# Up projections of the two branches: four PSUM banks, two low halves on another engine, a subtraction one tile later, and a later place for the residual rows

## The chip, the cores and the metric

The kernel runs on one core of a Trainium2 chip. Its engines work side by side, each through its own list of instructions in order: TensorE (PE: matmuls, which write to PSUM), VectorE (DVE), ScalarE (ACT), GpSimd (POOL) and SyncE (SP). They wait for one another by semaphores. DMAs are issued from SP's queue and from POOL's queue. PSUM has eight banks of 128 x 512 float32. The metric is the time of one execution on the device, in microseconds; three runs of the kernel before took 800.81 to 802.07 us, with a median of 801.13.

## What is computed

One decoder layer on x of 512 x 1024 in float32. After a norm, one wide projection gives the inputs of two branches: an mLSTM (`hm`, 512 x 512) and a sparse attention (`on`, 512 x 512), and two gates `gm` and `gn` of 512 x 1024. The branches are projected up, gated, added and projected by `w_out`; the result is added to x (the residual), normalised again and sent through a gated MLP with a short convolution. The part around the change:

```
y = jax.nn.sigmoid(gm + merge_gate_b[0]) * (hm @ w_up_m) \
    + jax.nn.sigmoid(gn + merge_gate_b[1]) * (on @ w_up_n)
x = x + y @ w_out
h2 = rmsnorm(x, norm2_w)
```

`w_up_m` and `w_up_n` are 512 x 1024, `w_out` is 1024 x 1024.

## The kernel before

**Products in three matmuls.** Every float32 operand of a large product is split into a high half in TensorE's rounded format (fp32r) and a low half, the rest. A product is H·h + H·l + L·h, three matmuls. So each weight has to be converted: `Weights.ensure(i)` (L71 and on) takes half i of a loaded chunk, writes its high half with a copy on ScalarE (L88), and the low half in one of two ways. In the usual way VectorE subtracts high from raw (L94). For halves listed in `W.on_dma`, ScalarE writes the negative of the high half (L91) and a DMA from POOL's queue adds the raw weights to it in place (L92). The second way takes more of ScalarE and a transfer, and nothing of VectorE.

**Order of the weights.** Chunks are loaded from SP's queue (L68) into two raw buffers in turn; a chunk is loaded as soon as `ensure` comes to the first half of the chunk before it, and waits on the queue until the buffer's last reader is done. For a half converted by DMA, that reader is the DMA. The converted halves lie in four buffers in turn. `w_up_n`, `w_up_m` and `w_out` have four, four and eight halves, and the text calls them UN0 to UN3, UM0 to UM3 and WO0 to WO7; two halves make a chunk. The list `PLAN` holds switches; `poolUN` is 2, so all four halves of `w_up_n` go the way with the DMA; those of `w_up_m` and `w_out` go through VectorE.

**Streams of projection work.** The order of all instructions on each engine is that of the program. A `Filler` takes a generator of matmul steps (three matmuls, valued at 650) and issues as many as the surrounding stage asks for, so that TensorE has products between the small operations of the other stages. An evacuation of a finished PSUM tile is put into the program two steps after the tile's last step (`after(2, ...)`).

**The two up projections.** `up_group` works through eight tiles m of 128 x 512, each of four steps, twelve matmuls; a pair of tiles needs one half of the weights. At the third step of every even tile it calls `ensure` for the half three places on. The `un` group runs beside the last head of the mLSTM: the products `mo` (L1136), which wait for `EA` (L1128), the norm of that head, then the sigmoids of `gn` on ScalarE (L1275, between two loads of function tables, L1271 and L1276), and, after 18 steps, the four transposes `mhT` (L1165). A `un` tile is evacuated by a multiply into `gn` (L741) on VectorE. The `un` group uses the two `pa` banks in turn. The `um` group then uses the two `psS` tiles in turn, which the mLSTM heads used before (two banks each, of which `um` takes the first).

**The merge.** `evac_um(m)` multiplies a `um` tile into `gm` (L1299), adds `gn` (L1300), both on VectorE (`umpool` is 0), copies to the high half `yH` on ScalarE (L1301), and subtracts for the low half `yL` on VectorE (L1302).

**What comes behind.** The PSUM pool of the stages so far is closed and a pool of eight single banks takes its place; a bank of it waits for the last reader of the old tile at that place. Each of the eight k-steps of `w_out` goes over four row tiles and two column halves: 24 matmuls into eight banks. The residual rows (four loads of 512 KB, L1289) and the weights of the second norm (L1291) are issued from POOL's queue ahead of the `um` group, into pages of the pool `outer`, which held the normalised input until the last `gn` product. Their sum with the `w_out` product (L1346), the norm and the MLP follow.

Of the kernel before, what the change touches and what calls it, by code (L numbers as in the profile page):

```python
# [15 lines left out]
P = 128  # L16
S = 512
D = 1024
NT = S // P
KD = D // P  # L20
# [77 lines left out]
def bcast(ap, n):  # L98
    return bass.AP(tensor=ap.tensor, offset=ap.offset, ap=[[0, P], [1, n]])
# [17 lines left out]
    "p_sc21": 0, "p_sc30": 0, "p_sc31": 1, "poolA": 2, "poolC": 0, "poolGM": 2, "poolGN": 2, "poolMO": 2,  # L117
    "poolMQK": 2, "poolMV": 0, "poolUM": 0, "poolUN": 2, "poolWO": 0, "q2_eb": 1, "q2_ex0": 0, "q2_ex1": 0,
# [10 lines left out]
def FL(key, default):  # L129
    return PLAN.get(key, default)  # L130


PD = dict(A=0, C=2, MV=2, GM=2, MO=2, MQK=2, GN=0, UN=0, UM=0, WO=0)
# [27 lines left out]
def body(ctx, tc, I, out, dbg=None):  # L161
    nc = tc.nc
    act, dve, pe, pool = nc.scalar, nc.vector, nc.tensor, nc.gpsimd
    ctx.enter_context(tc.manual_schedule())

    x = I["x"][0]
# [30 lines left out]
    def page(name, dt=F32):  # L197
        return ar.tile([P, 2048], dt, name=name, tag="pg", bufs=PG)
# [7 lines left out]
    def s4(name, dt=F32):  # L206
        return ar.tile([P, 1024], dt, name=name, tag="s4", bufs=6)
# [13 lines left out]
    def v4(tl):  # L221
        return tl[:, :2048].rearrange("p (k t) -> p k t", t=S)

    def act4(tiles, k, a=0, b=S):
        return v4(tiles[k // 4])[:, k % 4, a:b]

    T = {}
# [10 lines left out]
    W = Weights(nc, wpool, 2, 4)  # L238
# [17 lines left out]
    def add_feat(src, c0, nkt, width, per_half):  # L256
        s = src[:, c0:c0 + width].rearrange("(k p) n -> p k n", p=P)
        views = [lambda v, a=a: v[:, :, a:a + per_half] for a in range(0, width, per_half)]
        return W.add((nkt, width), [(lambda v: v, s)], views)
# [9 lines left out]
    F_UN = [i for c in range(0, 1024, 512) for i in add_feat(w_up_n, c, 4, 512, 256)]  # L269
    F_UM = [i for c in range(0, 1024, 512) for i in add_feat(w_up_m, c, 4, 512, 256)]  # L270
# [20 lines left out]
    W.on_pool = {T_B[c] for c in range(4) if FL(f"q2_pb{c}", (1, 0, 0, 0)[c])}  # L291
    for nm, ids in (("A", T_A), ("C", T_C), ("MV", T_MV), ("GM", F_GM), ("MO", F_MO), ("MQK", F_MQK), ("GN", F_GN),
                    ("UN", F_UN), ("UM", F_UM), ("WO", T_WO[:4])):
        W.on_dma |= set(ids[1:len(ids):2] if FL("pool" + nm, PD[nm]) == 1 else ids if FL("pool" + nm, PD[nm]) == 2 else [])
    for i in T_WO[4:]:
        W.dst[i] = page_r

# [137 lines left out]
    def after(n, fn):  # L435
        later.append([n, fn])

    def tick():
        ready = []
        for e in later:  # L440
            e[0] -= 1
        while any(e[0] <= 0 for e in later):
            n = next(i for i, e in enumerate(later) if e[0] <= 0)
            ready.append(later.pop(n)[1])
        for fn in ready:
            fn()
# [48 lines left out]
                yield 650  # L495
                tick()

    def up_group(ids, mH, mL, evac, nm, flag, bank=pa):
        for m in range(KD):
            acc = bank(f"{nm}{m}")[:, 0:512]  # L500
            W.ensure(ids[m // 2])
            H, L = W.hl[ids[m // 2]]
            w = slice((m % 2) * P, (m % 2) * P + P)
            for k in range(4):
                if k == 2 and m % 2 == 0:
                    W.ensure(ids[m // 2] + 3)
                pe.matmul(acc, H[:, k, w], mH[:, k, :], start=(k == 0), stop=False)
                pe.matmul(acc, H[:, k, w], mL[:, k, :], start=False, stop=False)
                pe.matmul(acc, L[:, k, w], mH[:, k, :], start=False, stop=(k == 3))
                if k == 3:  # L510
                    after(2, lambda m=m, acc=acc: evac(m, acc))
                    if m == KD - 1:
                        after(2, lambda: done.add(flag))
                yield 650
                tick()
# [227 lines left out]
    def proj_stream():  # L743
        yield from tok_group(T_C, 288, tok_accs("aC"), evac_c, "C")
        yield from tok_group(T_A, 512, tok_accs("aA"), evac_a, "A")
        T["mv1"] = lpage("mv1").rearrange("p (t h c) -> p t h c", t=NT, h=4)
        pool.memset(T["mv1"][:, :, :, P:P + 1], 1.0)
        yield from tok_group(T_MV, 512, tok_accs("aV"), evac_mv, "MV")
        T["gm"] = [v4(opage(f"gm{i}")) for i in range(2)]
        yield from feat_group(F_GM, gate_evac("gm", 0), "gm", "GM")  # L750
        T["mo"] = v4(page("mo"))
        yield from feat_group(F_MO, evac_mo, "mo", "MO")
        yield from feat_group(F_MQK, evac_conv, "mqk", "MQK")
        T["gn"] = [v4(page(f"gn{i}")) for i in range(2)]
        yield from feat_group(F_GN, gate_evac("gn", 8), "gn", "GN")

    fill = Filler(proj_stream(), flush)
# [330 lines left out]
    def mls_s(h):  # L1088
        r0 = slice((h % 2) * 64, (h % 2) * 64 + 64)
        mq = T["mq"][h // 2][r0]  # L1090
        A = psS(f"mA{h}")
        B = psS(f"mB{h}")
        mb = B[:, 0:512]
        pe.matmul(mb, sel[:, h, :], T["nHL"], start=True, stop=True)
        at = [A[:, 0:512], A[:, 512:896], B[:, 768:1024], B[:, 512:768]]
        for j in range(NT):
            ks = slice(j * P, (j + 1) * P)
            kh, kl = mq[:, 1, ks], mq[:, 3, ks]

            q0 = min(j, NT - 2) * P  # L1100
            qh, ql = mq[:, 0, q0:], mq[:, 2, q0:]
            pe.matmul(at[j], kh, qh, start=True, stop=False)
            pe.matmul(at[j], kh, ql, start=False, stop=False)
            pe.matmul(at[j], kl, qh, start=False, stop=True)
        return A[:, 0:896], B[:, 640:1024], mb
# [20 lines left out]
    def mls_m(sc, ee):  # L1126
        EA, EB, et = ee
        dve.scalar_tensor_tensor(EA, sc[0], 0.125, EA, op0=ALU.mult, op1=ALU.mult)  # L1128
        dve.scalar_tensor_tensor(EB, sc[1], 0.125, EB, op0=ALU.mult, op1=ALU.mult)
# [119 lines left out]
    for i in range(2):  # L1249
        for z in range(2):  # L1250
            g = T["gm"][i][:, 2 * z:2 * z + 2, :]
# [9 lines left out]
    for h in range(4):  # L1261
        if h < 3:
            mid = (lambda: mls_s(h + 1), lambda n: mls_e(h + 1, n), mls_x)
        else:
            mid = (lambda: None, lambda n: None, lambda n: None)
        fill(FL(f"mb{h}", 1000))
        hs, sc, ee = mls_b(h, ee[2], mid)
        if h == 3:
            fill.until(done, "GN")
            fill = Filler(up_group(F_UN, T["onH"], T["onL"], evac_un, "un", "UN"), flush)  # L1270
            act.preload_act_table_set("sigmoid_and_others")  # L1271
            for i in range(2):
                for z in range(2):
                    g = T["gn"][i][:, 2 * z:2 * z + 2, :]
                    act.activation(g, g, AF.Sigmoid)  # L1275
            act.preload_act_table_set(LNEXP)  # L1276
        fill(FL(f"mc{h}", 5000))
        mls_c(h, hs)
        if h < 3:
            fill(FL(f"md{h}", 2000))  # L1280
            mls_m(sc, ee)
# [3 lines left out]
    x1p = [opage(f"x1_{i}") for i in range(2)]  # L1285
    x1d = dram.tile([S, D], F32, name="x1d")
    x1 = [x1p[t // 2][:, (t % 2) * 1024:(t % 2) * 1024 + 1024] for t in range(NT)]
    for t in range(NT):
        pool.dma_start(x1[t], x[t * P:(t + 1) * P, :])  # L1289
    nw2 = s4("nw2")  # L1290
    pool.dma_start(nw2, bcast(I["norm2_w"], D))  # L1291


    yH = [page(f"yH{i}", F32R) for i in range(2)]
    yL = [lpage("yL0", F32R), page("yL1", F32R)]

    def evac_um(m, a):
        g = T["gm"][m // 4][:, m % 4, :]
        dve.tensor_mul(g, g, a)  # L1299
        (pool if m < FL("umpool", 5) else dve).tensor_add(g, g, T["gn"][m // 4][:, m % 4, :])  # L1300
        act.activation(act4(yH, m), g, AF.Copy)  # L1301
        dve.tensor_sub(act4(yL, m), g, act4(yH, m))  # L1302

    fill = Filler(up_group(F_UM, T["hmH"], T["hmL"], evac_um, "um", "UM", psS), flush)
    fill(1e9)
    ps_cm.close()

# [6 lines left out]
    acc = {t: [pf(f"wo{t}{c}") for c in range(2)] for t in range(NT)}  # L1314

    def wo(i, t):
        H, L = W.hl[T_WO[i]]
        for c in range(2):
            mm3(acc[t][c], act4(yH, i, t * P, (t + 1) * P), act4(yL, i, t * P, (t + 1) * P),
                H[:, 0, c * 512:(c + 1) * 512], L[:, 0, c * 512:(c + 1) * 512], i == 0, i == KD - 1)  # L1320

    for i in range(4):
        W.ensure(T_WO[i])
        for t in range(NT):
            if t == 2:
                W.ensure(T_WO[i] + 3)
            wo(i, t)
    W.ensure(T_WO[7])
    h2H = [opage_r(f"h2H{i}") for i in range(2)]
    h2L = [opage_r(f"h2L{i}") for i in range(2)]  # L1330
# [144 lines left out]
    acc = {}  # L1475
# [53 lines left out]
    for j in range(2, NJ - 2):  # L1529
# [7 lines left out]
        if 4 <= j < 8:  # L1537
            t = j - 4
# [102 lines left out]
```

## Time and profile before

| | us |
|---|---|
| median of three runs | 801.13 |
| the profiled execution, own time | 799.94 |
| its span, first to last instruction | 798.2 |
| TensorE busy | 776.9 (97%) |
| VectorE busy | 469.7 (59%) |
| ScalarE busy | 373.0 (47%) |
| GpSimd busy | 211.1 (26%) |

Busy time is the sum of an engine's instructions, loads of weights into TensorE's array apart. Starts are in us from the first instruction. In a row of the timeline the square bracket says how long the engine stood before the instruction and what released it; several equal instructions in a row are merged, with their count behind an x. The duration of a matmul is longer than the distance to the next one, since they overlap; the pace is read from starts. Instructions of VectorE and ScalarE overlap by a little too.

### The profile page before, as it was taken

The page shows a single profiled execution, that of the slowest core. Times are in us where ns is not written, and L with a number is a line of the kernel's source. Part 1 is how long each engine was busy: PE and PEld are TensorE (multiplying, and loading weights), DVE is VectorE, ACT ScalarE, POOL GpSimd, SP SyncE. Part 2 cuts the span into 40 slices and gives each one's busy share as a digit, 9 for nine tenths or more (in the row PEclk, how much of TensorE's full clock was granted, in tenths as well). Part 3 has the DMA queues.
Part 4 walks back from the last instruction along what each step waited for, and adds up shares of the span by engine and source line. Part 5 has one row for each costly group of instructions (what it writes and reads, how often), then busy time and mean ns, then how long its engine had stood idle before and what let it go on. Part 6 is the DMA issues. An engine that isn't in the chain of part 4 may idle for free.

```text
span 798.2 us, 10535 instructions
## 1 busy us (share of the span) xinstructions
PE 776.9 (97%) x4037; PEld 640.9 (80%) x4037; DVE 469.7 (59%) x825; ACT 373.0 (47%) x629; POOL 211.1 (26%) x219
## 2 busy tenths in 40 slices
PE   8999989999999999988999999999999999999998
PEld 5897878778788878866778998888888888888886
DVE  5476875686565654534764545555545544466865
ACT  6353546645565596571343343343343343355541
POOL 5320121220111122121000009855554444200600
PEclk9999999999999999999999999999999999999999
DMA  7884158665555567348343427675454444485472
GB/s 234 290 222 133 25 135 132 109 113 96 106 106 107 106 106 129 83 106 263 105 151 125 148 106 290 241 260 209 182 188 181 188 158 159 168 306 177 144 233 93
DMA packets 94371, 127.98 MB, mean 160 GB/s; under 512 B 6479, under 2 KB 73199, under 8 KB 92912
## 3 DMA queue, kind: packets, MB, share of 16 engines
q1 hardware_dynamic: 63054, 91.64, 34.3%
q0 software_dynamic: 31264, 35.66, 21.6%
q8 instruction: 32, 0.52, 0.3%
q14 instruction: 19, 0.16, 0.1%
q10 hardware_dynamic: 2, 0.00, 0.0%
HBM read 94.79 MB, written 15.73 MB: 138 GB/s over the span
## 4 chain that ended last, share of the span: by engine, by line
PE 79%; DVE 9%; ACT 6%; DMA 3%; issue 2%; SPq 0%; DVEq 0%; ACTq 0%
PE ff L1356 10%; PE ff L1357 10%; PE ff L1358 10%; PE P L426 4%; PE P L427 4%; PE P L425 4%; PE on L946 2%; PE ptp L935 2%; PE wo L425 2%; PE wo L426 2%; PE wo L427 2%; PE gm L487 1%; PE gm L489 1%; PE gm L488 1%; PE sp L905 1%
## 5 line engine op out<-in xcount | busy, mean ns | idle before, releaser
L94 DVE TENSOR_TENSOR whl<-raw,whl 128x1024 fp32r<-128x1024 f32 (+1 forms) x110 | 138.9, 1276 | 146.7 <-ACT whl L88 146.7
L88 ACT ACTIVATE whl<-raw 128x1024 fp32r<-128x1024 f32 (+2 forms) x144 | 144.8, 1013 | 125.7 <-PE ff L1358 57.0
L1356 PE MATMUL ff<-h2H,whl 128*128 128x512 f32 (+1 forms) x384 | 142.8, 372 | 0.0
L1357 PE MATMUL ff<-h2L,whl 128*128 128x512 f32 (+1 forms) x384 | 142.6, 371 | 0.0
L1358 PE MATMUL ff<-h2H,whl 128*128 128x512 f32 (+1 forms) x384 | 142.6, 371 | 0.0
L92 POOL DMA_DIRECT2D whl<-raw x32 | 46.2, 1444 | 198.5 <-ACT whl L91 190.3
L1358 PEld LDWEIGHTS ff<-h2H,whl 128*128 128x128 f32 x384 | 72.3, 188 | 12.6
L1356 PEld LDWEIGHTS ff<-h2H,whl 128*128 128x128 f32 x384 | 72.3, 188 | 12.5
L1357 PEld LDWEIGHTS ff<-h2L,whl 128*128 128x128 f32 x384 | 72.3, 188 | 12.3
L920 ACT ACTIVATE P<-sp,nmx 128x128 f32<-128x128 f32 (+3 forms) x64 | 33.1, 524 | 36.7 <-DVE nmx L911 36.4
L1408 ACT ACTIVATE ct<-ct 128x512 f32<-128x512 f32 x22 | 14.0, 634 | 54.4 <-DVE ct L1406 54.4
L911 DVE TENSOR_REDUCE nmx<-sp 128x2 f32<-128x256 f32 (+3 forms) x32 | 26.2, 818 | 17.9 <-PE sp L908 17.8
L426 PE MATMUL P<-whl,g 128*128 128x512 f32 x88 | 34.2, 389 | 0.0
L427 PE MATMUL P<-whl,g 128*128 128x512 f32 x88 | 34.2, 389 | 0.0
L425 PE MATMUL P<-whl,g 128*128 128x512 f32 x88 | 34.2, 389 | 0.0
L1406 DVE SCALAR_TENSOR_TENSOR ct<-ff,vcol,ct 128x511 f32<-128x511 f32 (+1 forms) x44 | 32.8, 744 | 2.5 <-ACT ct L1404 1.7
L91 ACT ACTIVATE whl<-raw 128x1024 fp32r<-128x1024 f32 x32 | 33.6, 1050 | 0.0
L1414 ACT ACTIVATE g<-ct 128x512 fp32r<-128x512 f32 x22 | 13.9, 634 | 37.0 <-DVE ct L1418 21.9
L235 DVE COPY P<-ptp 128x256 f32<-128x256 f32 (+1 forms) x32 | 17.7, 554 | 19.3 <-PE ptp L935 19.2
L1415 DVE TENSOR_TENSOR g<-ct,g 128x512 fp32r<-128x512 f32 x22 | 15.4, 699 | 22.0 <-ACT g L1414 22.0
L425 PE MATMUL wo<-whl,yH 128*128 128x512 f32 x64 | 25.2, 394 | 1.8 <-DVE gm L1299 1.8
L487 PE MATMUL gm<-hTH,whl 128*128 128x512 f32 x64 | 26.6, 416 | 0.0
(400 smaller groups left out, 1788.6 us busy)
## 6 DMA issues: line engine op xcount, KB each, us to landing
raw<-in_ffn_w_up_dram SPq DMA_DIRECT2D x22, 1024.0 KB, 5.0
raw<-in_w_in_dram SPq DMA_DIRECT2D x16, 1024.0 KB, 5.0
whl<-raw POOLq DMA_DIRECT2D x32, 512.0 KB, 5.7
st<-in_ffn_w_down_dram SPq DMA_DIRECT2D x11, 1024.0 KB, 6.9
td<-st POOLq DMA_DIRECT2D x11, 1024.0 KB, 4.1
raw<-td SPq DMA_DIRECT2D x22, 512.0 KB, 5.4
raw<-in_ffn_w_down_dram SPq DMA_DIRECT2D x11, 512.0 KB, 4.4
raw<-in_w_out_dram SPq DMA_DIRECT2D x4, 1024.0 KB, 11.0
```

The lines of the kernel that those rows point to most:

```text
L88: nc.scalar.activation(h, src, AF.Copy)
L91: nc.scalar.activation(l, src, AF.Copy, scale=-1.0)
L92: nc.gpsimd.dma_start(l, src, accum_op=ALU.add)
L94: (nc.gpsimd if n in self.on_pool else nc.vector).tensor_sub(l, src, h)
L425: pe.matmul(o, aH, bH, start=start, stop=False)
L426: pe.matmul(o, aH, bL, start=False, stop=False)
L427: pe.matmul(o, aL, bH, start=False, stop=stop)
L487: pe.matmul(acc, H[:, k, :], hh, start=(k == 0), stop=False)
L920: act.activation(Pv[:, y], sv[:, y], AF.Exp, bias=nmx[:, y:y + 1], accum_out=den[:, y:y + 1])
L1356: pe.matmul(acc[:, a:b], H[:, k, :], hh, start=(k == 0), stop=False)
L1357: pe.matmul(acc[:, a:b], H[:, k, :], hl, start=False, stop=False)
L1358: pe.matmul(acc[:, a:b], L[:, k, :], hh, start=False, stop=(k == KD - 1))
```

## The change

Five edits. First, `poolUN` becomes 3, a new value: the first two halves of `w_up_n` keep the DMA, UN2 and UN3 get their low half from VectorE. Second, `up_group` takes its PSUM tile for even m from `pa` and for odd m from `psS`, in both groups, so each goes over four banks. Third, UN3 is converted ahead of the sigmoids of `gn`, where it was behind them, by its own call of `ensure`. Fourth, `evac_um(m)` subtracts for the tile before, m - 1, and for the last tile both. Fifth, the loads of the residual rows and of the second norm's weights are issued in the program inside the first four steps of `w_out`, a row tile after each, where they were ahead of the `um` group; their pages are allocated at the old place.

```
-    "poolMQK": 2, "poolMV": 0, "poolUM": 0, "poolUN": 2, "poolWO": 0, ...
+    "poolMQK": 2, "poolMV": 0, "poolUM": 0, "poolUN": 3, "poolWO": 0, ...

-        W.on_dma |= set(ids[1:len(ids):2] if FL("pool" + nm, PD[nm]) == 1 else ids if FL("pool" + nm, PD[nm]) == 2 else [])
+        W.on_dma |= set(ids[1:len(ids):2] if FL("pool" + nm, PD[nm]) == 1 else ids if FL("pool" + nm, PD[nm]) == 2
+                       else ids[:2] if FL("pool" + nm, PD[nm]) == 3 else [])

-    def up_group(ids, mH, mL, evac, nm, flag, bank=pa):
+    def up_group(ids, mH, mL, evac, nm, flag):
         for m in range(KD):
-            acc = bank(f"{nm}{m}")[:, 0:512]
+            acc = (psS if m % 2 else pa)(f"{nm}{m}")[:, 0:512]

             fill = Filler(up_group(F_UN, T["onH"], T["onL"], evac_un, "un", "UN"), flush)
+            W.ensure(F_UN[3])
             act.preload_act_table_set("sigmoid_and_others")

-    for t in range(NT):
-        pool.dma_start(x1[t], x[t * P:(t + 1) * P, :])
     nw2 = s4("nw2")
-    pool.dma_start(nw2, bcast(I["norm2_w"], D))

         act.activation(act4(yH, m), g, AF.Copy)
-        dve.tensor_sub(act4(yL, m), g, act4(yH, m))
-
-    fill = Filler(up_group(F_UM, T["hmH"], T["hmL"], evac_um, "um", "UM", psS), flush)
+        if m:
+            y_low(m - 1)
+        if m == KD - 1:
+            y_low(m)
+
+    def y_low(m):
+        dve.tensor_sub(act4(yL, m), T["gm"][m // 4][:, m % 4, :], act4(yH, m))
+
+    fill = Filler(up_group(F_UM, T["hmH"], T["hmL"], evac_um, "um", "UM"), flush)

             wo(i, t)
+        pool.dma_start(x1[i], x[i * P:(i + 1) * P, :])
+        if i == 1:
+            pool.dma_start(nw2, bcast(I["norm2_w"], D))
```

## Rows read from the trace of the kernel before

**Rows 1.** TensorE by stretch: us, busy (matmuls), granted clock, DMA share, GB/s.
```profile
345.00:403.00 58.00, 49.15 (x207) 0.97 0.50 153
379.60:383.10 3.50, 3.48 (x9) 0.52 0.83 293
403.00:798.00 395.00, 391.30 (x1829) 1.00 0.53 187
```
**Rows 2.** Waits of TensorE from 335 to 440: us in total, times, longest.
```profile
PE un L507 <- DVE gn L741: 3.8, 3, 2.5
PE um L507 <- DVE gm L1299: 3.3, 2, 2.2
...
PE mo L1136 <- DVE EA L1128: 0.6, 1, 0.6
```
**Rows 3.** Timeline of TensorE, 344 to 403: start, us, instruction, idle before it.
```profile
344.80 0.47 PE L507 MATMUL un<-onH,whl 128*128 128x512 f32 x1
...
361.27 0.60 PE L1165 MATMUL mhT<-ident,hs 128*128 128x128 f32 x4
...
371.83 0.39 PE L507 MATMUL um<-hmH,whl 128*128 128x512 f32 x1
...
379.62 0.77 PE L507 MATMUL um<-hmH,whl 128*128 128x512 f32 x1 [2.18 <-DVE gm L1299]
...
399.02 0.39 PE L425 MATMUL wo<-whl,yH 128*128 128x512 f32 x1
...
400.83 0.39 PE L427 MATMUL wo<-whl,yL 128*128 128x512 f32 x1
402.99 0.50 PE L425 MATMUL wo<-whl,yH 128*128 128x512 f32 x1 [1.76 <-DVE gm L1299]
```
**Rows 4.** Timeline of ScalarE: UN2's first pass, UM0's, a merge copy, WO0's.
```profile
340.61 1.04 ACT L88 ACTIVATE whl<-raw 128x1024 fp32r<-128x1024 f32 x1
...
356.82 1.04 ACT L88 ACTIVATE whl<-raw 128x1024 fp32r<-128x1024 f32 x1
...
382.94 0.63 ACT L1301 ACTIVATE yH<-gm 128x512 fp32r<-128x512 f32 x1 [2.08 <-DVE gm L1300]
383.48 1.05 ACT L88 ACTIVATE whl<-raw 128x1024 fp32r<-128x1024 f32 x1
```
**Rows 5.** Timeline of VectorE: `EA` ahead of `mo`, and the first two `un` evacuations.
```profile
341.35 1.08 DVE L1128 SCALAR_TENSOR_TENSOR EA<-mA,EA 128x896 f32<-128x896 f32 x1
...
350.78 1.29 DVE L741 TENSOR_TENSOR gn<-gn,un 128x512 f32<-128x512 f32 x2 [0.18 <-ACT gn L1275]
```
**Rows 6.** Timeline of VectorE in the merge, 378.5 to 386.
```profile
378.79 0.68 DVE L1299 TENSOR_TENSOR gm<-gm,um 128x512 f32<-128x512 f32 x1
379.50 0.69 DVE L1300 TENSOR_TENSOR gm<-gm,gn 128x512 f32<-128x512 f32 x1
380.89 0.69 DVE L1302 TENSOR_TENSOR yL<-gm,yH 128x512 fp32r<-128x512 f32 x1 [0.70 <-ACT yH L1301]
381.50 0.68 DVE L1299 TENSOR_TENSOR gm<-gm,um 128x512 f32<-128x512 f32 x1
...
384.56 1.23 DVE L94 TENSOR_TENSOR whl<-raw,whl 128x1024 fp32r<-128x1024 f32 x1 [0.26 <-ACT whl L88]
385.70 0.68 DVE L1299 TENSOR_TENSOR gm<-gm,um 128x512 f32<-128x512 f32 x1
```
**Rows 7.** POOL's queue, UN1, UN3, residual rows; landing of L92's 32 DMAs.
```profile
339.93 1.29 POOL L92 DMA_DIRECT2D whl<-raw  x1 [1.55 <-ACT whl L91]
...
357.29 1.28 POOL L92 DMA_DIRECT2D whl<-raw  x1 [13.11 <-ACT whl L91]
358.04 2.71 POOL L1289 DMA_DIRECT2D x<-in_x_dram  x4
...
DMA to landing us min/median/max: 4.4/5.7/9.6
```
**Rows 8.** DMA issues from 363 to 364: KB each, us to landing.
```profile
raw<-in_w_up_m_dram SPq DMA_DIRECT2D x1, 1024.0 KB, 10.7
```

More of the change, by code (lines that the diff above doesn't have):

```diff
@@ L117 @@
     "p_sc21": 0, "p_sc30": 0, "p_sc31": 1, "poolA": 2, "poolC": 0, "poolGM": 2, "poolGN": 2, "poolMO": 2,
-    "poolMQK": 2, "poolMV": 0, "poolUM": 0, "poolUN": 2, "poolWO": 0, "q2_eb": 1, "q2_ex0": 0, "q2_ex1": 0,
+    "poolMQK": 2, "poolMV": 0, "poolUM": 0, "poolUN": 3, "poolWO": 0, "q2_eb": 1, "q2_ex0": 0, "q2_ex1": 0,
     "q2_ex2": 1, "q2_ex3": 0, "q2_na": 1, "q2_nb": 1, "q2_nc": 1, "q2_pb0": 1, "q2_pb1": 1, "q2_pb2": 0,
```

## The prediction

> **What bounds the kernel now.** The table of stages comes first [rows 1]: TensorE is busy 391.30 of the 395 us from 403 to the end, but only 49.15 of the 58 us from 345 to 403, the two up projections and the first products of `w_out`. So what this change can give back lies in those 58 us. The waits of TensorE say who holds it there [rows 2]: the `un` products wait 3.8 us for the evacuation of an older bank (`gn`, L741), the `um` products 3.3 us for theirs (L1299), and `mo`, just ahead, 0.6 us for `EA`. The timeline of TensorE gives the places [rows 3]: `un` begins at 344.80, `um` at 371.83, `um` stands 2.18 us until 379.62, the first `w_out` product is issued at 399.02, and its fourth bank has to wait until 402.99 for the last `um` evacuation. From there on TensorE runs through, so **the start of that matmul, 402.99, is the point that counts**: what moves it moves the end. The nine matmuls from 399.02 to 400.83 give the pace, 1.81/8 = 0.227 us each, 2.72 us for a tile of twelve, 5.44 us for two. Eight tiles need 21.8 us; `un` took 27.03.
>
> **UN2 (third half of `w_up_n`): low half on VectorE.** Its high half runs on ScalarE from 340.61 for 1.04 us [rows 4], and so the new subtraction can start at 341.7. By program order it stands before `EA`, which today starts at 341.35 [rows 5]. One such subtraction takes 1.14 us until the next instruction (384.56 to 385.70 [rows 6]). `EA` then starts at 341.7 + 1.14 = 342.84, which is 1.5 us later, and `mo` waits for just that instruction. Bounds: 0, if something else were late by as much, and 1.5; I take 1.5, since the wait on `EA` is already there. `un` begins at 346.3. ScalarE loses its second pass over UN2, which nobody waits for.
>
> **UN3: before the sigmoids, low half on VectorE.** Its high half costs ScalarE one more pass of 1.0 us ahead of the sigmoids' table load. The first evacuation of `un` today starts at 350.78, released by a sigmoid [rows 5]; it comes at 350.78 + 1.5 + 1.0 = 353.3. With two banks that would stall the third tile. With **four banks** the fifth tile is the first to need it, at 346.3 + 4 x 2.72 = 357.2: four microseconds of cover. The next two evacuations stand behind the subtraction for UM0, whose pass on ScalarE starts at 356.82 [rows 4] + 1.5 - 1.0 (a pass for UN3 is gone) = 357.3; with 1.05 for it, 1.14 for the subtraction and 1.29 for both evacuations [rows 5] they are through by 360.8, and the seventh tile wants the first of them at 363. So I count all three `un` waits as gone. Queued behind UN3's new subtraction on VectorE is nothing but these evacuations. `un` ends at 346.3 + 21.8 + 0.6 (the four `mhT` transposes [rows 3] and a slow first matmul) = 368.7, against 371.83.
>
> **UN3's DMA was also a plug.** The transfer that subtracts for UN3 is issued at 357.29 and lands about 5.7 us later, the median of its kind [rows 7], and only then is the raw buffer free for the second half of `w_up_m`, which lands 10.7 us after that, with the residual rows in flight beside it [rows 8]. 357.3 + 5.7 + 10.7 = 373.7, and the conversion of UM2 then delays the whole of `um`: that is the 2.18 us. Afterwards the buffer is free when VectorE has done UN3, about 353.3; even at 10.7 us the load lands at 364, before ScalarE asks for it.
>
> **Residual rows.** In program order they move behind the first `w_out` products, but they sit on the queue of POOL, and what stands ahead of them there goes away: today they go out at 358.04 right behind UN3's transfer [rows 7], and the last entry left is UN1's, issued at 339.93. Their pages held the normalised input, free after the last `gn` product, so I expect them **earlier**, at about 342 to 345, not later. They are then beside UN1's transfer (needed at 346.3 + 5.4 = 351.7; the slowest of the kind took 9.6 us [rows 7], so 349.5) and the first load of `w_up_m`. Cost taken: 0, hidden by that slack and by the sigmoids; bounds: 0 to what rival E gives. If they do go out late, they lie beside `w_out` loads, with more than 20 us until they are added, also 0.
>
> **The merge, subtraction one tile behind.** Per two tiles VectorE today needs 385.70 - 378.79 = 6.91 us [rows 6]. The 0.70 us waits for ScalarE's copy go. But the conversion of the next `w_out` half stands on ScalarE behind the second copy, and VectorE waits for it in order. From rows: multiply to add 0.71; add to the older subtraction 0.61 (estimate: as subtraction to multiply); subtraction 0.61; multiply 0.71; add 0.69; then the copy starts 0.04 later, 0.54 to the conversion [rows 4], 1.08 until VectorE takes it up, 1.14 for the low half: 6.13 us. That is 0.8 less than before but still over TensorE's 5.44, so VectorE falls behind by 0.7 per two tiles.
>
> **The sum.** `um` starts at 368.7. The multiply of its second tile starts at 368.7 + 5.44 + 0.16 = 374.3; the third's comes 0.71 + 0.69 + 0.04 + 0.54 + 1.08 + 1.14 = 4.20 later at 378.5, the fifth's at 384.6, the seventh's at 390.8, and the eighth's, 1.93 after that, at 392.7 ends at 393.4. With four banks `um` itself doesn't wait (tile seven starts at 385.0, its bank free at 379.2). TensorE is through `um` at 390.5; it waits about a microsecond for the seventh tile's bank (391.5) and its fourth `w_out` bank starts at 391.5 + 2.04 + 0.1 = 393.6, where the last multiply has just made room. 402.99 - 393.6 = **9.4 us**. Behind it every load and conversion is released by work that comes 9 us earlier too, and rows 1 leave no wait there to grow. Own time of the profiled execution: 799.94 (span 798.2 and 1.74 around it) - 9.4 = 790.5; the median of the runs stands 1.19 above that execution, hence **791.7**.
>
> Its own ends: VectorE never behind and UN2 free gives 390.5 + 2.04 - 1.5 = 391.0, 12.0 us, 789.1; a merge that stays at 6.91 loses 3 x 0.78 = 2.3, 7.1 us, 794.0.
>
> **Rivals.**
> A, as above, 791.7.
> B, the clock falls at the new wait. Ahead of `mo` TensorE would stand 0.6 + 1.5 = 2.1 us, as long as the 2.18 before 379.62, behind which the granted clock was 0.52, half of 2.4 GHz, and nine matmuls took 3.50 us in place of 2.04 [rows 1]. For it: the likeness. Against it: the same stretch holds a longer wait, 2.5 us [rows 2], and its 58 us show a mean of 0.97, all of which that one fall explains (3.5 x 0.48 = 1.7 of 58). Price 1.5: 793.2. The Trainium skill, "TensorE: Matmul & The Clock Gate", section "A second HAM failure mode: psum-queue depth-cycling", says that going round through banks with small idle times in each turn lets the clock swing between its two levels. By that rule the change, which goes round four banks, would lose more than once; the trace has one fall in all of the bank-cycling stretch.
> C, the series of copy, conversion and subtraction keeps the merge at its old pace: 794.0. For it: 1.65 us of ScalarE now stand where VectorE can't work; against it: the sum by rows.
> D, the four banks do not do what they say: a wait on weights takes their place, and only UN3's earlier buffer and the shorter merge pay: 3.8 less, 795.5. Against it: UN1 and UN2 are there long before.
> E, the other side: the early residual rows (2 MB, and 0.5 MB for the norm's weights) choke UN1's transfer. It decides from 351.7 on, where the third `un` tile wants UN1; each microsecond later is one lost, and the `w_up_m` load is queued behind the same buffer. Break-even at 361. At three times the slowest row, 28.8 us, UN1 lands at 368.7: 17.0 lost, 9.4 won, 808.7. For it: a load beside these rows took 10.7 us. Against it: UN1 is issued 2 us ahead of them. The Trainium skill, "DMA: Bandwidth & Descriptors", section "Issuing engines are not separate DMA queues", says that transfers of all engines run on the same 16 DMA engines and interleave, so being first in POOL's queue does not keep UN1 clear.
>
> **Chances.** A 0.70, B 0.12, C 0.08, D 0.04, E 0.06, half of that beyond break-even by more than 0.2% and half within. About 0.2%, 1.6 us, is what a measurement here can tell from no change. Faster: 0.94; same 0.03; slower 0.03. The range runs from near A's lower end to a little past C: 789.4 to 795.0.
>
> **What would show it.** Right: no `un` or `um` matmul waits for a bank; `mo` waits some 2 us; the second `w_up_m` load is issued near 353; the residual rows go out before 350; two merge tiles take about 6.1 us; a wait of about 1 us at the first `w_out` matmuls; the fourth bank near 393.6. Wrong: a third `un` tile that waits for UN1, a clock under 1 after 342, or any TensorE wait after 394 that was not there.

## The result, and the profile after

The changed kernel takes **792.45 us** (median of four runs, 792.17 to 793.33) against 801.60 for the kernel before in the same comparison (800.81 to 802.62): a ratio of 0.9887, 95% interval 0.9870 to 0.9904, so 9.15 us faster. The forecast was 791.7. The profiled execution of the changed kernel took 793.33, its span is 791.6.

TensorE by stretch, the columns as in [rows 1]:
```profile
345.00:394.00 49.00, 48.00 (x217) 0.97 0.47 163
394.00:792.00 398.00, 393.25 (x1838) 1.00 0.53 186
```
The boundary, 394, is where the forecast put the fourth `w_out` bank; the bank starts at 396.09 (below), so what took 58 us from 345 on now takes 51. TensorE is idle for 1.0 us of that, not 8.9; the longer wait ahead of `mo` comes before 345. Its waits from 335 to 440 stand against [rows 2]:
```profile
PE mo L1137 <- DVE EA L1129: 2.1, 1, 2.1
PE wo L426 <- DVE gm L1298: 1.0, 1, 1.0
```
No `un` or `um` product waits for a bank. The wait ahead of `mo` has grown from 0.6 to 2.1, and one new wait of 1.0 stands in the first `w_out` products. The timeline of TensorE gives the places that answer to [rows 3]:
```profile
342.37 0.39 PE L490 MATMUL gn<-hTH,whl 128*128 128x512 f32 x1
344.81 2.47 PE L1137 MATMUL mo<-mv,EA 128*128 128x129 f32 x10 [2.06 <-DVE EA L1129]
...
348.68 0.47 PE L508 MATMUL un<-onH,whl 128*128 128x512 f32 x1
...
371.04 0.39 PE L508 MATMUL um<-hmH,whl 128*128 128x512 f32 x1
...
393.96 0.47 PE L426 MATMUL wo<-whl,yH 128*128 128x512 f32 x1 [1.00 <-DVE gm L1298]
...
396.09 0.39 PE L426 MATMUL wo<-whl,yH 128*128 128x512 f32 x1
```
`un` takes 371.04 - 348.68 = 22.4 us (27.0 before), `um` eight times 2.72 = 21.8 (27.2 before); the fourth `w_out` bank, the point that counts, starts at 396.09 (402.99 before). But `mo` itself is slow: its ten first products take 2.47 us. The same engine in stretches of 2 us (us, busy, granted clock, DMA share, GB/s) shows why:
```profile
344.00:346.00 2.00, 1.19 (x6) 0.71 1.13 142
346.00:348.00 2.00, 2.00 (x11) 0.50 0.99 372
348.00:350.00 2.00, 2.00 (x13) 0.94 0.92 354
350.00:352.00 2.00, 2.00 (x11) 1.00 0.96 352
```
Behind the wait of 2.06 us the granted clock falls to 0.50, that is from 2.4 to 1.2 GHz, and `mo` pays for it: from its start to the first `un` product it is 3.87 us, against 344.80 - 342.58 = 2.22 before, where its rows are these:
```profile
341.61 0.39 PE L489 MATMUL gn<-hTH,whl 128*128 128x512 f32 x1
342.58 1.35 PE L1136 MATMUL mo<-mv,EA 128*128 128x129 f32 x10 [0.58 <-DVE EA L1128]
```
From 350 on the clock is full. Counted from the last `gn` product, ahead of the change, the fourth `w_out` bank comes 396.09 - 342.37 = 53.72 us later, against 402.99 - 341.61 = 61.38 before: 7.66 us less by these two traces.

VectorE, the rows that answer to [rows 5] and [rows 6]:
```profile
342.44 1.23 DVE L94 TENSOR_TENSOR whl<-raw,whl 128x1024 fp32r<-128x1024 f32 x1 [0.25 <-ACT whl L88]
343.58 1.08 DVE L1129 SCALAR_TENSOR_TENSOR EA<-mA,EA 128x896 f32<-128x896 f32 x1
...
355.61 1.28 DVE L742 TENSOR_TENSOR gn<-gn,un 128x512 f32<-128x512 f32 x2
...
380.89 0.68 DVE L1298 TENSOR_TENSOR gm<-gm,um 128x512 f32<-128x512 f32 x1
...
385.87 1.23 DVE L94 TENSOR_TENSOR whl<-raw,whl 128x1024 fp32r<-128x1024 f32 x1 [1.04 <-ACT whl L88]
387.01 0.68 DVE L1298 TENSOR_TENSOR gm<-gm,um 128x512 f32<-128x512 f32 x1
```
UN2's new subtraction stands right ahead of `EA`. In the merge the 0.70 waits for the copy are gone, one of 1.04 for ScalarE's conversion has come, and two tiles take 387.01 - 380.89 = 6.12 us, not 6.91.

POOL's queue, against [rows 7]:
```profile
340.68 1.29 POOL L92 DMA_DIRECT2D whl<-raw  x1 [1.55 <-ACT whl L91]
341.45 1.66 POOL L1333 DMA_DIRECT2D x<-in_x_dram  x2
...
343.08 1.60 POOL L1333 DMA_DIRECT2D x<-in_x_dram  x2
```
The residual rows, later in the program, go out 16.6 us earlier (341.45 against 358.04). The second half of `w_up_m`, by SP's queue, goes out and lands (KB, us) so, against the 10.7 us of [rows 8]:
```profile
355.64 0.37 SPq L68 DMA_DIRECT2D raw<-in_w_up_m_dram  x1
```
```profile
raw<-in_w_up_m_dram SPq DMA_DIRECT2D x1, 1024.0 KB, 5.2
```
And one difference is not the change's. The first projection's first product waits for `hTH` on ScalarE, 1.68 us where it was 1.00, and so this execution is 0.7 us late from the start (before, that product started at 11.24). ScalarE is late because it stands, in order ahead of `hTH`, at the conversion of the first weights, whose load lands later (ScalarE before, ScalarE after, the product after):
```profile
6.89 1.06 ACT L88 ACTIVATE whl<-raw 128x1024 fp32r<-128x1024 f32 x1 [0.65 <-DMA raw<-in_w_in_dram]
...
7.58 1.06 ACT L88 ACTIVATE whl<-raw 128x1024 fp32r<-128x1024 f32 x1 [1.32 <-DMA raw<-in_w_in_dram]
...
11.92 0.51 PE L426 MATMUL aB<-whl,hTH 128*128 128x512 f32 x1 [1.68 <-ACT hTH L422]
```

### The profile page after: what moved, and what is told of

Same layout as the page of the kernel before. It is cut to its first block, busy times and chain, and to the rows that moved or that the text cites. A ratio compares the mean times of both kernels' runs of the same rounds, so it can differ in the third digit from the quotient of the medians.

```text
span 791.6 us, 10531 instructions
## 1 busy us (share of the span) xinstructions
PE 775.5 (98%) x4037; PEld 641.7 (81%) x4037; DVE 471.5 (60%) x827; ACT 371.1 (47%) x627; POOL 208.5 (26%) x217
## 4 chain that ended last, share of the span: by engine, by line
PE 84%; DVE 8%; ACT 4%; issue 1%; DMA 1%; SPq 0%; DVEq 0%; ACTq 0%
PE ff L1366 10%; PE ff L1365 10%; PE ff L1364 10%; PE P L427 4%; PE P L428 4%; PE P L426 4%; PE on L947 2%; PE ptp L936 2%; PE wo L426 2%; PE wo L428 2%; PE wo L427 2%; PE gm L488 1%; PE gm L490 1%; PE gm L489 1%; PE sp L906 1%
## 5 line engine op out<-in xcount | busy, mean ns | idle before, releaser
L94 DVE TENSOR_TENSOR whl<-raw,whl 128x1024 fp32r<-128x1024 f32 (+1 forms) x112 | 141.4, 1275 | 139.1 <-ACT whl L88 139.1
L92 POOL DMA_DIRECT2D whl<-raw x30 | 43.6, 1454 | 183.7 <-ACT whl L91 175.6
L91 ACT ACTIVATE whl<-raw 128x1024 fp32r<-128x1024 f32 x30 | 31.5, 1050 | 0.0
L1355 POOL DMA_DIRECT2D x1d<-x x4 | 2.1, 536 | 95.1 <-DVE x L1354 95.1
```

Of the source, the lines that this page charges most:

```text
L92: nc.gpsimd.dma_start(l, src, accum_op=ALU.add)
L94: (nc.gpsimd if n in self.on_pool else nc.vector).tensor_sub(l, src, h)
```

## The experiments

The theory: the 9.15 us are the plug taken out (UN3 early on VectorE), then four banks, then the shorter merge, less a clock fall of 1.5 us behind `mo`'s wait. The rivals: that the fall is an accident of one execution; that one part alone does it all; that the residual rows matter. "The changed kernel" below is the mean of its two repeats' medians, 793.2, unless a repeat of the same comparison is named. The first four kernels were timed together (the kernel before: 801.14, 800.41 to 803.10, 11 runs), the next four (801.17, 799.80 to 804.19, 18 runs), and the last two (801.46, 800.24 to 802.34, 7 runs).

**1. The changed kernel once more, no edit.**

> The changed kernel itself, once more, as the yardstick of its neighbours: about 9.2 us below the kernel before (792.4 against 801.6). In its first trace TensorE stood 2.06 us ahead of mo and the clock then fell to half for about 3.5 us; theory: that fall is set off by the wait but doesn't come in every execution, so single times spread over about 1.5 us. Rival: the fall comes each time, and the times lie within 0.5 us of each other.

793.23 us (792.41 to 793.31), ratio 0.9893 [0.9878, 0.9908]. `mo` waits 2.04 us, and the clock is 0.79, 0.50 and 0.86 in the 2 us stretches from 344 to 350. The mean granted clock is 0.997 or 0.998 in each of the four runs, so the fall is no accident of one execution. Nor does it come in every one: of the first set's four runs one, of 792.24, has a mean clock of 1.0. The times here spread over 0.9 us, between the 1.5 of the theory and the 0.5 of the rival.

**2. UN2's low half by DMA, as before**: `EA` is not delayed.
```diff
-  else ids[:2] if FL("pool" + nm, PD[nm]) == 3 else [])
+  else ids[:3] if FL("pool" + nm, PD[nm]) == 3 else [])
```


> The changed kernel, but UN2 gets its low half by DMA again (only UN3 goes through VectorE). Theory: the subtraction ahead of EA costs the 1.5 us that mo waits longer, and the fall of the clock behind that wait another 1.5 where it comes. So mo's wait goes from 2.1 back to about 0.6 us, un starts 1.5 us earlier at least, no clock under 1 between 342 and 350, and the whole is 1.5 to 3.0 us faster than the changed kernel (789.4 to 790.9). Rival: something else is late by as much (UN2's transfer, which now holds the raw buffer of the second half of w_up_m and stands ahead of the residual rows on POOL's queue), and the time stays within 0.5 us of the changed kernel.

790.65 (790.22 to 790.97), 0.9863 [0.9848, 0.9878], 2.6 faster than the repeat beside it. The waits of TensorE:
```profile
PE wo L426 <- DVE gm L1298: 1.0, 1, 1.0
PE mo L1137 <- DVE EA L1129: 0.6, 1, 0.6
PE un L508 <- DVE gn L742: 0.5, 1, 0.5
```
`mo`'s wait is back at 0.6, and the granted clock is 1.00 in each stretch from 336 to 404 and in the mean of all four runs. The parts add up: 1.5 for the subtraction, 1.65 for the clock, less 0.5 for a new `un` wait, is 2.65. So a subtraction of 1.14 us, put ahead of `EA`, costs 2.6 us.

**3. Two banks for each group**, the rest changed.
```diff
-    def up_group(ids, mH, mL, evac, nm, flag):
+    def up_group(ids, mH, mL, evac, nm, flag, bank=pa):
-            acc = (psS if m % 2 else pa)(f"{nm}{m}")[:, 0:512]
+            acc = bank(f"{nm}{m}")[:, 0:512]
-    ... evac_um, "um", "UM"), flush)
+    ... evac_um, "um", "UM", psS), flush)
```


> The changed kernel with two banks per up projection, as before (un in pa, um in psS). Theory, from the sum of the prediction: un's third tile waits for the first evacuation behind the sigmoids (about 2.2 us), its fifth for one behind UM0's subtraction (0.8); um then starts some 3 us later and the merge follows it: about 2.6 us slower than the changed kernel, with un waits of 3 us in the trace. Rival: the banks are the main thing and without them most of the 9.2 us is gone (5 us or more slower). Other rival: VectorE paces anyway and the banks are worth nothing (within 0.5 us).

795.62 (795.19 to 797.06), 0.9929 [0.9914, 0.9943], 2.4 slower than the repeat.
```profile
PE un L508 <- DVE gn L742: 2.8, 3, 1.9
PE mo L1137 <- DVE EA L1129: 2.1, 1, 2.1
PE um L508 <- DVE gm L1298: 0.3, 1, 0.3
PE wo L426 <- DVE gm L1298: 0.2, 1, 0.2
```
The three `un` waits for a bank come back with 2.8 us; the wait at `w_out` shrinks from 1.0 to 0.2 since VectorE has less to catch up on. In its profiled execution the clock does not fall behind `mo`'s 2.06 (the mean of the other runs, 0.997 to 1.0, suggests that it does in some). So the length of a wait alone does not decide.

**4. The merge's subtraction in its own tile**, the rest changed.
```diff
-        if m:
-            y_low(m - 1)
-        if m == KD - 1:
-            y_low(m)
+        y_low(m)
```


> The changed kernel with the merge's subtraction back in its own tile. Theory: two tiles take 6.9 us of VectorE again in place of 6.1, the last multiply comes 3 x 0.78 = 2.3 us later, and so does the fourth bank of w_out: 2.2 to 2.3 us slower than the changed kernel, with the wait ahead of the first w_out products up from 1.0 to over 3 us. Rival: the four banks hide the slower merge (within 0.5 us).

795.85 (795.03 to 796.76), 0.9929 [0.9916, 0.9943], 2.6 slower. Two tiles take 386.65 - 379.74 = 6.91 us again, and the wait is at `w_out`:
```profile
PE wo L426 <- DVE gm L1298: 2.6, 1, 2.6
PE mo L1137 <- DVE EA L1129: 2.0, 1, 2.0
```
I had expected over 3 us of wait; it was 2.6, and the clock falls behind it (stretches of 2 us as above), which makes up the rest; behind `mo`'s wait the clock held in this execution:
```profile
394.00:396.00 2.00, 1.61 (x6) 0.82 0.00 0
396.00:398.00 2.00, 2.00 (x6) 0.50 0.00 0
398.00:400.00 2.00, 2.00 (x9) 0.83 0.00 0
```

**5. The residual rows at their old place in the program**, the rest changed.
```diff
+    for t in range(NT):
+        pool.dma_start(x1[t], x[t * P:(t + 1) * P, :])
     nw2 = s4("nw2")
+    pool.dma_start(nw2, bcast(I["norm2_w"], D))
...
-        pool.dma_start(x1[i], x[i * P:(i + 1) * P, :])
-        if i == 1:
-            pool.dma_start(nw2, bcast(I["norm2_w"], D))
```


> The changed kernel with the residual rows and the norm's weights back at their old place in the program, ahead of the um group. Theory: POOL has nothing between the two places, so the move is none on its queue (only the norm's weights change places with the last two row loads); the rows go out at about 341.5 as in the changed kernel, and the time is the same within 0.5 us. Rival: the place in the program counts, the rows now collide with other loads, and it is a microsecond or more slower.

792.61 (791.98 to 793.84), 0.9887 [0.9868, 0.9906]: the same as the changed kernel within the interval. POOL issues them at 342.01, and not at 358.04 [rows 7]:
```profile
342.01 2.70 POOL L1291 DMA_DIRECT2D x<-in_x_dram  x4
```
What made them early is that UN3's transfer is gone from ahead of them (in experiment 7, also at the old place, they go out at 341.19); the edit itself does nothing to the time.

**6. Four banks alone**, on the kernel before.
```diff
-            acc = bank(f"{nm}{m}")[:, 0:512]
+            acc = (psS if m % 2 else pa)(f"{nm}{m}")[:, 0:512]
```


> The kernel before with four banks per up projection as the only edit. Theory: the un waits on banks (3.8 us in the trace of before) go, but the second half of w_up_m still waits for UN3's DMA, UM2 is still converted at about 374, and the merge on VectorE starts and runs as before, 6.9 us per two tiles; TensorE only arrives earlier and waits there instead: 0, within 0.7 us of the kernel before. Rival: the waits on banks are worth what they show, 3 to 4 us faster.

802.66 (802.07 to 803.85, 12 runs), 1.0015 [1.0004, 1.0026]: not faster, and by the medians 1.5 slower, a little outside what I had expected.
```profile
PE wo L425 <- DVE gm L1299: 3.6, 1, 3.6
PE um L507 <- DVE gn L741: 3.1, 1, 3.1
PE un L509 <- DMA whl<-raw: 1.0, 1, 1.0
```
TensorE runs through `un` until it waits for UN3's DMA itself, and stands again at the third tile of `um`, whose bank VectorE empties late. VectorE shows why:
```profile
376.44 1.23 DVE L94 TENSOR_TENSOR whl<-raw,whl 128x1024 fp32r<-128x1024 f32 x1 [10.23 <-ACT whl L88]
377.58 1.28 DVE L741 TENSOR_TENSOR gn<-gn,un 128x512 f32<-128x512 f32 x2
```
It stands 10.23 us at UM2's low half, with the evacuations in order behind it, because the second load of `w_up_m` still goes out behind UN3's transfer and still takes 10.7 us, as in [rows 8]. The bank is free at 377.58 + 0.7, and the product starts at 378.40. The clock falls behind both long waits (us, busy, granted clock, DMA share, GB/s):
```profile
378.00:380.00 2.00, 1.59 (x4) 0.50 0.00 0
...
402.00:404.00 2.00, 2.00 (x6) 0.50 0.00 0
```
and the fourth bank starts at 405.18, against 402.99 + 1.16 of later start. The kernel before falls once here [rows 1]. The mean clock, 0.990 to 0.994 in all twelve runs against 0.994 to 1.000 for the kernel before, says the same. More banks only move the wait along while the load behind it is late.

**7. UN2 and UN3 early on VectorE alone**, on the kernel before.
```diff
-    "poolUN": 2
+    "poolUN": 3
...
+            W.ensure(F_UN[3])
             act.preload_act_table_set("sigmoid_and_others")
```
(with the line of the change that reads the flag's value 3)

> The kernel before with UN2 and UN3 through VectorE and UN3 ahead of the sigmoids as the only edits; two banks and the old merge stay. Theory: the raw buffer is free some 10 us earlier, the second load of w_up_m is issued near 353 to 356, um starts near the end of un (371 to 373) without the wait for UM2, and the merge starts 4.4 us earlier at its old pace: 4.4 us faster than the kernel before, 2.9 if the clock falls behind mo's longer wait. Rival: without the banks nothing is gained (within 0.7 us), since un waits on its two banks.

798.35 (797.80 to 800.56), 0.9959 [0.9944, 0.9974]: 2.8 faster than before, the lower of the two figures.
```profile
PE un L508 <- DVE gn L742: 2.8, 3, 1.9
PE mo L1137 <- DVE EA L1129: 2.1, 1, 2.1
PE wo L426 <- DVE gm L1301: 1.8, 1, 1.8
PE um L508 <- DVE gm L1301: 1.1, 1, 1.1
```
The 2.18 us in the middle of `um` are gone, and two tiles of the merge still take 6.9 us; the clock falls behind `mo` (0.50 from 346 to 348) and again behind the 1.8 at `w_out` (0.72 from 402 to 404, 0.50 from 404 to 406). This execution is the slowest of the seven, 2.2 us above their median.

With 3 and 4 this gives the parts by medians: the plug out, 2.8, with what UN2 costs taken off; with the merge 801.14 - 795.62 = 5.5; with the banks instead 801.14 - 795.85 = 5.3; with both 7.9. So 2.8, 2.7 for the merge and 2.5 for the banks add up to 8.0, near the 7.9, if the plug goes first; without that the banks are worth nothing, and the merge without it was not run. The parts are rough: the interval of each ratio is about 1.2 us either way, and falls of the clock are mixed into them. From the last `gn` product to the end the profiled executions take 456.6 us before (one fall), 456.7 here (two), 451.1 in 3 (none), 450.8 in 4 (one) and 449.2 in the changed kernel (one).

**8. A version that the traces point to**: UN2 by DMA as in 2, and for the `w_out` halves in the merge ScalarE's conversion ahead of the merge's copies, while VectorE's low half stays where it is.
```diff
+    def release(self):
+        held, self.held = self.held, None
+        for f in held or ():
+            f()
...
-                (nc.gpsimd if n in self.on_pool else nc.vector).tensor_sub(l, src, h)
+                def low(e=..., l=l, src=src, h=h): e.tensor_sub(l, src, h)
+                if self.held is None: low()
+                else: self.held.append(low)
...   # up_group, for UM and m > 0
+                if k == 0 and m % 2 == 0: W.held = []; W.ensure(ids[m // 2] + 3)
-                if k == 2 and m % 2 == 0: W.ensure(ids[m // 2] + 3)
+                if k == 2 and m % 2 == 0: W.release()
```


> The changed kernel with UN2 by DMA, and in the um group the high half of the next w_out weights put on ScalarE ahead of the merge copy, its low half on VectorE left where it was. Theory: VectorE no longer waits 1.05 us per two tiles for that high half; two tiles take about 5.1 us, less than TensorE's 5.44, the wait of 1.0 us ahead of the first w_out products goes, and the whole is 1.0 us faster than the kernel with UN2 by DMA alone (789.6). Rival: ScalarE's conversion now delays the merge copy or waits for a buffer, and the time stays or gets worse.

**789.72** (789.21 to 790.08), 0.9849 [0.9831, 0.9866], 0.9 faster than 2 and 3.5 faster than the changed kernel; against experiment 5, timed beside it, 2.9. The kernel of 2 was timed in another set, and the two intervals overlap; but by the traces too, from the last `gn` product to the end, it is 445.3 us here and 446.4 there. The wait of 1.0 at `w_out` is gone. VectorE in the merge:
```profile
379.72 0.69 DVE L1316 TENSOR_TENSOR gm<-gm,um 128x512 f32<-128x512 f32 x1 [0.37 <-PE um L528]
...
385.16 0.69 DVE L1316 TENSOR_TENSOR gm<-gm,um 128x512 f32<-128x512 f32 x1 [0.36 <-PE um L528]
```
Two tiles take 5.44 us, TensorE's pace (5.1 was expected of VectorE alone), and what VectorE waits for is now TensorE. What is left for TensorE is `mo`'s 0.6 and one `un` wait of 0.6.

**9. The wait filled**: nine products ahead of `mo` on data that has long been there, in the changed kernel.
```diff
+        if h == 3:
+            full = pa("full")
+            for k in range(9):
+                pe.matmul(full, identr, <identr, four times side by side>, start=True, stop=True)
         hs, sc, ee = mls_b(h, ee[2], mid)
```


> The changed kernel with nine matmuls of 512 columns more, whose product nobody reads, put on TensorE between the last gn product and mo: 9 x 0.227 = 2.04 us in the 2.06 us in which it stood. They take nothing away from mo's wait for EA, so un starts no earlier by that; only the idle time goes. Theory: the clock's fall is set off by that idle time and costs some 1.5 us of mo and un where it comes: no clock under 1 between 342 and 352, mo back from 3.9 to 2.3 us, and 1.0 to 1.5 us faster than the changed kernel (791.2 to 791.9). Rival: the fall belongs to mo's small matmuls themselves; the clock falls all the same and the time is that of the changed kernel or a little more.

792.04 (791.57 to 793.55), 0.9882 [0.9866, 0.9899], 1.1 faster than the repeat beside it (10).
```profile
344.60 2.20 PE L1271 MATMUL full<-identr 128*128 128x512 f32 x9
346.81 1.35 PE L1137 MATMUL mo<-mv,EA 128*128 128x129 f32 x10
...
349.04 0.48 PE L508 MATMUL un<-onH,whl 128*128 128x512 f32 x1
```
`mo` starts 2.44 us after the last `gn` product is issued (344.37), exactly as in the changed kernel (344.81 - 342.37), and then takes 349.04 - 346.81 = 2.23 us in place of 3.87; the clock is 1.00 from 336 to 402. So the 1.65 us are the clock's, and the idle time brings the fall. Experiments 3 and 4 agree, whose traces have the same wait and no fall behind it: from the last `gn` product to the first of `un` they take 4.67 and 4.65 us, this one 4.67, the changed kernel 6.31. From the last `gn` product to the end it is 447.4 us against 449.2, 1.8 less; the extra tile also takes a turn of the `pa` banks, and the wait at `w_out` is now 0.8 and stands at the fourth bank. Between the medians it is 1.1: one of the four runs has a mean clock of 0.997 (the others 1.0), so a fall whose place is not known, and the profiled one is late ahead of the edit, with its last `gn` product 2.0 us behind that of the changed kernel.

**10. The changed kernel a third time, beside 9.**

> The changed kernel as the yardstick of the run beside it: 792.4 to 793.3 as in its two sets so far, with the clock's fall behind mo's wait in its trace. Rival to the theory that the fall is common: its trace shows none.

793.17 (792.75 to 793.99), 0.9899 [0.9885, 0.9914], `mo`'s wait 2.06 and the clock down again behind it.

## Why the prediction was right, and where not

**The point that counts** was right: from the fourth bank to the end of the span it is 395.2 us before and 395.5 after, and no new wait stands behind it.

**UN2's 1.5 us** were right. The last `gn` product is issued at 342.37 (341.61 before, mostly the late start), and `EA` starts 343.58 - 341.35 = 2.23 later: 0.76 and 1.47.

**The step that failed is the clock behind `mo`** (rival B, given 0.12). It came in each of the three profiled executions of the changed kernel, and two of the three medians, 793.23 and 793.17, stand on B's 793.2 and not on A's 791.7. With it came one of the prediction's own signs of being wrong, a clock under 1 after 342. The argument against B was one longer wait, 2.5 us, behind which the clock had held. One counterexample was too little, and the trace of before held one for the other side as well, the 2.18 that the prediction names. Of the seven waits of 2.0 to 2.1 us ahead of `mo` in these profiles the clock fell behind five (the changed kernel three times, experiments 5 and 7) and held behind two (3 and 4). The rows at hand, one such wait of each kind, gave about even odds, and with them 792.5 as the middle of A and B. The price, 1.5, was right: 1.65 by the trace.

That the forecast is still near the first median, 792.45, is in part luck: that set is the fastest of the three, and two distances between a profiled execution and its runs' median took 2.1 us off the miss. The forecast added 1.19 us, the distance of the profiled execution of before from its runs' median; the profiled execution after is the slowest of its four, 0.9 above their median. For the profiled execution itself it said 790.5, and that took 793.33. By the trace the fourth bank is 2.49 later than forecast (396.09 against 393.6): 0.76 late start, 1.65 clock, 0.08 the rest. By medians the gain is 9.15, 7.9 and 8.3 in the three comparisons, where 9.4 was forecast and 7.9 is 9.4 less 1.5.

**UN3, four banks, the `un` waits** came as worked out: no wait, 22.4 us. The first evacuation was put at 353.3 and came at 355.61; less late start and clock that is 353.2. The Trainium skill's rule on going round through banks ("TensorE: Matmul & The Clock Gate", section "A second HAM failure mode: psum-queue depth-cycling") did not bite: with four banks the clock is 1.00 in each stretch from 350 to 404. No product of `un` or `um` stood idle in its turn here, so the case that the page describes did not arise. In these traces the clock fell behind single long waits only.

**The plug** was there. The load goes out at 355.64 (about 353 forecast, and again the 2.4 us between) and lands in 5.2 us instead of 10.7: the residual rows, issued by 344.7 and 9.4 us in flight in the median, are down by then. The shorter flight was not needed: in experiments 2 and 8 the load went out at 352.99 and 352.34, took 10.1 and 10.2 us again and so landed near 363, against 374 before, and no `um` product waited. What pays is the earlier release. Alone with UN2 it is worth 2.8 us (experiment 7), and it is what lets the banks pay (experiment 6).

**The residual rows** came early, as forecast, and cost nothing: UN1's transfer, issued at 340.68 with the rows 0.8 us behind it (not the 2 of the prediction), landed in 6.4 us, where the same transfer took 5.1 before. Rival E, which needed 28.8, had the direction right and the size far off.

**The merge** was right to 0.01 us (6.12 for 6.13), with the wait on ScalarE's conversion in the place of the copy's, and so was the 1.0 us at `w_out`. Rival C is refuted by the same row; its price, 2.3, was 2.6 in experiment 4, where a smaller wait and a clock fall make it up. Rival D is refuted by TensorE's waits; its price, 795.5, is what experiment 3 without the four banks took, 795.62.

**Not settled**: what decides whether the clock falls behind a wait of some 2 us. Its length does not, and nothing else that was compared here separates the two kinds. The fall does not start at a fixed distance either: the first ten products of `mo`, 1.35 us at full clock, took 2.47, 2.17 and 2.32 us in the three executions of the changed kernel, and 1.74 in experiment 5.

## What to carry to other kernels

Before a stall is bought off by putting work ahead of an instruction that the bounding engine waits for, add to the delay what a clock fall costs behind it (here 1.65 us for 1.5 us of delay), even where one wait of that length in the trace has gone unpunished; a few idle products avoid it (experiment 9); products that are needed later may do as well, which was not tried. More buffers paid here only when the load that refills them was on time: take out the late load first, then count buffers. And where two engines work in series on one tile, look at the order on both queues: moving ScalarE's conversion ahead of its copies took the last 0.7 us per two tiles (6.12 to 5.44) that the shifted subtraction had left.

## What was not expected of the hardware

The granted clock held behind one wait of 2.06 us (experiment 3) and fell behind another of the same length, at the same place in nearly the same program. It fell behind one of 1.77 at `w_out` in experiment 7, and held behind one of 1.94 at `un` in that same execution.

Executions of one kernel differ by up to 4.4 us (the kernel before, 799.80 to 804.19), with mean clocks of 0.994 to 1.000. The profiled ones differ from the first projection's first product on, which starts between 11.24 and 12.46 us. In all twelve that is 2.99 to 3.05 us after ScalarE starts its second conversion of the first weights, released by the load of `w_in`: so it is that load that sets the start. From that product to the last `gn` product it is another 330.4 to 332.1 us. For differences of a microsecond the traces have to be compared from a common instruction ahead of the change, not from the start of the span.
